# Other places for the operands and rounded weights of a decoder block's up-projection, in the order in which the last column pair uses them

## The chip, the core and the metric

The kernel runs on one core of one Trainium2 chip. The metric is device time in microseconds (us), the median over several executions; lower is better. The core's engines are named as in the profile: PE (TensorE, with its weight loads apart as PEld), DVE (VectorE), ACT (ScalarE), POOL (GpSimd) and SP (SyncE, which issues the DMAs). Each works through its own list of instructions in order and waits on semaphores for the others.

## The reference

One layer of a decoder block over 1024 tokens of width 1024: two token mixers in parallel, a residual and a layer norm, a gated feed-forward with a short causal convolution, a second norm, a gated embedding and a third norm.

```python
x = layer_norm(ALPHA * x + mixed, ln1_g, ln1_b)
h = causal_dwconv(x @ w_up, conv_w, conv_b)          # w_up: 1024 x 5632; three taps
h_gate, h_val = jnp.split(h, 2, axis=-1)             # 2816 columns each
ffn = (jax.nn.silu(h_gate) * h_val) @ w_down         # w_down: 2816 x 1024
x = layer_norm(ALPHA * x + ffn, ln2_g, ln2_b)
```

The change touches the product `x @ w_up`.

## The kernel before

**Two parts of each number.** A float32 operand is split into a rounded high part (`wh`, made by ACT at L101) and the remainder (`wl`, made by POOL or DVE at L106). A product of two operands is three matmuls: high by high, high by low, low by high (`mm3`, all at L155).

**Seven products in place of eight.** `x @ w_up` is cut in two by two blocks, and each pair of column blocks (a gate block of 128 columns and a value block) is computed by seven products of sums of blocks. There are 22 pairs, f = 0 to 21. For each product j there are an operand `XS[j]`, made once from the normed tokens in `x_sets` by `right_operands`, and for each pair a weight operand `W[j]`, made in `w_sets` by `left_operands`. A product is 4 by 3 matmuls on 128x512, a pair 84.

**How the weights are made.** Two raw blocks arrive by DMA, in tiles named `wr` for even pairs and `ar` for odd ones, four quarters a11, a12, a21, a22. `left_operands` forms on DVE (L164) the sums a11 = a11 - a21, a21 = a21 + a22, a22 = a22 - a11 and at last a12 = a12 - a22, all in place, and splits between them: product 0 is a11 as loaded, 5 is a22 as loaded, 1 is a22 after its sum, 2 is a21, 3 is a11 after its sum, 4 is a12 as loaded, 6 is a12 after its sum. Because the sums are in place, a sum must wait until the splits that read the old quarter are done: a12 waits for product 4's split, a22 for product 5's. From the second pair on every low part is made by POOL (`UE`), every high part by ACT.

**How a pair runs.** The functions in `up` are called in the order p0, p1, then p6 and the conv of the pair before, p5, p2, p3, p4, conv1. Results are collected in PSUM banks A to D (`ch`) and added into two tiles `h` (DVE at L1043, ACT at L1050 and L1074). p3 and p6 accumulate onto banks that p1 and p2 began, and must wait until DVE has read them. `conv` then scales on ACT (L1085), adds two taps on DVE (L1087), applies Silu on ACT (L1089), and POOL multiplies gate and value (L164 on `cv`, here called the gate product), whose result goes to DRAM (L1097).

**Places.** Tiles live in pools with a fixed number of places; a new tile of a pool's tag takes a place that an earlier tile of that tag has left, and its first write waits until the readers of that earlier tile are done. `bpool` has four places for `XS`, `apool[0]` two, `xpool` one. The weights' parts have four places each (`wh` and `wl`) in `wq` and three each in `fp`. When the 22 pairs are done, `xpool`, `wq`, `apool[0]` and `bpool` are closed, and `wpool` and `upool` of the down-projection are opened over the same bytes: units `wu` (weights) and `au` (activations), whose first writes wait for what lay there.

**What sets the order.** The code records instructions; a scheduler then sets the order on each engine, taking instructions as they become ready by its own reckoning and places as they become free. So other places can give another order.

Of the kernel before, what the change touches and what calls it, by code (L numbers as in the profile page):

```python
# [9 lines left out]
F32R = mybir.dt.float32r  # L10
# [7 lines left out]
P = 128  # L18
# [4 lines left out]
HALF = 512  # L23
# [17 lines left out]
def hybrid_block(ctx: ExitStack, tc: tile.TileContext, x, p, w_in, w_gate_up, b_gate, g_gla, w_gla,  # L41
# [5 lines left out]
    x, p, out = x[0], p[0, 0], out[0]  # L47
# [7 lines left out]
    def pool(name, bufs=1, space=bass.MemoryType.SB, stack=ctx, **kw):  # L55
        return stack.enter_context(tc.tile_pool(name=name, bufs=bufs, space=space, reuse_waits="tile", **kw))
# [5 lines left out]
    apool = [pool("acta", 2, stack=sega), pool("acta2", 2, stack=sega2, side="right")]  # L62
# [27 lines left out]
    def nm(s):  # L90
        uid[0] += 1
        return f"{s}_{uid[0]}"
# [122 lines left out]
    def quad(a):  # L215
        return a.rearrange("p (a b) -> p a b", b=P)
# [39 lines left out]
    def run(steps):  # L256
        for f in steps:
            f()
# [64 lines left out]
    with ExitStack() as mix:  # L323
# [65 lines left out]
        with ExitStack() as c1:  # L389
# [69 lines left out]
            def score_step(t, h):  # L459
                W = (t + 1) * P  # L460
                nch = 1 if W <= HALF else 2
                cw = W // nch
                sc = score[t]
# [219 lines left out]
        with ExitStack() as c3:  # L683
# [61 lines left out]
            def logit_steps(h, r):  # L745


                def one(i):
                    def f():
                        if i == 0:  # L750
                            PB[h, r] = tp.tile([P, 2 * r + 2, 2, 2, P], F16, name=nm("pt"), tag=f"pt{r}")
                        t, g = 2 * r + i, r // 2
                        W = (t + 1) * P
                        nch = 1 if W <= HALF else 2
                        cw = W // nch
                        qs = slice((t - g * 4) * P, (t - g * 4 + 1) * P)
# [83 lines left out]
    bpool = pool("actb", 4, stack=sega)  # L840
# [105 lines left out]
    segd, segk = ExitStack(), ExitStack()  # L946
    xpool = pool("xset", stack=segx)
    open_residual([x[t * P:(t + 1) * P, :] for t in range(NT)], 5)
    XS = [bpool.tile([P, 2, 4, HALF], F32R, name=nm("xs"), tag="B") for _ in range(4)]
    with ExitStack() as c1:  # L950
        lp = pool("ln1", stack=c1)
        gb1 = load_gb(lp, ln1_g, ln1_b)
        SPREAD, XE, XA = (1, 3), ('GVGVGVG', 'GVGVGVG', 'GGGVGGG', 'VVGVVGV'), ('VVVV', 'VVVV', 'VVVV', 'VVVG')

        def x_sets(i, xf):

            if i == 0:
                XS.extend(apool[0].tile([P, 2, 4, HALF], F32R, name=nm("xs"), tag="A") for _ in range(2))
                XS.append(xpool.tile([P, 2, 4, HALF], F32R, name=nm("xs"), tag="X"))
            cs = slice(i * P, (i + 1) * P)  # L960

            def put(j, src):
                split(XS[j][:, 0, :, cs], XS[j][:, 1, :, cs], quad(src), "A", XE[i][j])
            b11, b21, b12, b22 = xf
            run(right_operands(b11, b12, b21, b22, put, XA[i]))

        xfs = {}

        def fin1(t, nseg):
            layer_norm(t, nseg, gb1, EPS, t in SPREAD)  # L970
            r = RS["res"][t]
            tap(f"x1_{t}", r)
            xf = xfs.setdefault(t // 2, [])
            for g in range(2):
                pt = bank("mm" if t >= 4 else "pt", (P, 4, P))
                xq = lp.tile([P, HALF], F32, name=nm("xq"), tag="xq", bufs=5)
                xf.append(xq)
                for k in range(4):
                    n = g * 4 + k
                    turn_tile(pt[:, k], r[:, n * P:(n + 1) * P])  # L980
                S.activation(quad(xq), pt, AF.Copy)
            if t % 2:
                x_sets(t // 2, xf)
            nc.sync.dma_start(d_x1[t], r)

        def mixed(ps, rvs, *_):
            for j, rv in enumerate(rvs):
                V.scalar_tensor_tensor(rv, rv, ALPHA, ps[:, j], ALU.mult, ALU.add)

        tm_phase(FOURS, lambda c, *e: wload(wout_v, 0, KT, [c], *e),  # L990
                 lambda un, t, ps: tm_tile(un, tok(mT, t), ps),
                 mixed, fin1)
# [5 lines left out]
    with ExitStack() as c1:  # L998
        psum_banks(c1, "d", ch=8)
        fp = pool("ffwork", stack=c1)  # L1000
        rawp = pool("raws", stack=segd, side="right")
        wk = pool("upwork", stack=segk, side="right")
        UE, UE0, US = 'GGGGGGG', 'VVGVVGV', 'VVVV'
        nset = [0]

        def blocks(f):

            return (NF + f, f) if f < NF - 1 else (f, NF + f)

        def w_sets(f):  # L1010
            raw = []
            for c in blocks(f):
                if f % 2:
                    raw.append(rawp.tile([P, 6, 256], F32, name=nm("ar"), tag="ar", bufs=3)
                               .rearrange("p a b -> p (a b)")[:, :1024])
                else:
                    raw.append(wp.tile([P, 1024], F32, name=nm("wr"), tag="wr", bufs=2))
                nc.sync.dma_start(raw[-1].rearrange("p (k c) -> p k c", k=KT), wup_v[:, :, c * P:(c + 1) * P])
            W = []
            for _ in range(7):  # L1020
                n = nset[0] % 7
                nset[0] += 1
                pl, nb = (wq, 4) if n < 4 else (fp, 3)
                W.append([pl.tile([P, 512], F32R, name=nm(x), tag=x, bufs=nb) for x in ("wh", "wl")])
            run(left_operands(raw[1][:, :512], raw[1][:, 512:], raw[0][:, :512], raw[0][:, 512:],
                              lambda j, src: split(*W[j], src, "A", (UE if f else UE0)[j]), US))
            return [[quad(t) for t in w] for w in W]

        def up(f):

            W = w_sets(f)
            st, out_ = {}, {}

            def prod(ps, j, start):
                for k in range(4):
                    mm3(ps, (W[j][0][:, k], W[j][1][:, k]), (XS[j][:, 0, k], XS[j][:, 1, k]), start and k == 0, k == 3,
                        not start)  # L1040

            def plus(out, a, b):
                V.tensor_tensor(out=out, in0=a, in1=quad(b), op=ALU.add)  # L1043

            def p0():
                st["A"] = bank("ch")
                prod(st["A"], 0, True)
                st["h"] = [wk.tile([P, L], F32, name=nm("h"), tag=f"h{i}", bufs=2) for i in range(2)]
                st["hv"] = [h.rearrange("p (a g q) -> p g a q", g=2, q=P) for h in st["h"]]
                S.activation(st["hv"][1][:, 0], quad(st["A"]), AF.Copy)  # L1050

            def p1():
                st["B"] = bank("ch")
                prod(st["B"], 1, True)
                plus(st["hv"][0][:, 1], st["hv"][1][:, 0], st["B"])

            def p5():
                st["C"] = bank("ch")
                prod(st["C"], 5, True)

            def p2():
                st["D"] = bank("ch")
                prod(st["D"], 2, True)

            def p3():
                prod(st["B"], 3, False)
                s1, u3 = st["hv"][1][:, 0], st["hv"][1][:, 1]
                plus(u3, s1, st["B"])
                plus(s1, u3, st["C"])
                plus(u3, u3, st["D"])  # L1070

            def p4():
                prod(st["A"], 4, False)
                S.activation(st["hv"][0][:, 0], quad(st["A"]), AF.Copy)  # L1074

            def p6():
                prod(st["D"], 6, False)
                o = st["hv"][0][:, 1]
                plus(o, o, st["D"])

            def conv(i):
                c = blocks(f)[1 - i]
                h = st["h"][i]
                o = out_[c // NF] = wk.tile([P, L], F32, name=nm("cv"), tag="cv", bufs=3)
                S.activation(o, h, AF.Identity, bias=cbias[:, c:c + 1], scale=cw[:, 2, c:c + 1])  # L1085
                for d in (1, 2):
                    V.scalar_tensor_tensor(o[:, d:], h[:, :L - d], cw[:, 2 - d, c:c + 1], o[:, d:], ALU.mult, ALU.add)  # L1087
                if c < NF:
                    S.activation(o, o, AF.Silu)  # L1089

            def conv1():
                conv(1)

            def conv0():
                conv(0)
                sums(out_[0], out_[0], out_[1], ALU.mult, "G")
                nc.sync.dma_start(d_act[f // 6][:, f % 6], out_[0])  # L1097
            return p0, p1, p5, p2, p3, p4, conv1, p6, conv0

        late = []  # L1100
        for f in range(NF):
            p0, p1, p5, p2, p3, p4, conv1, *rest = up(f)
            run([p0, p1, *late[:1], p5, *late[1:], p2, p3, p4, conv1])
            late = rest
        late[0]()
        last_conv = late[1]
# [262 lines left out]
```

## Time and profile before

| what | value |
|---|---|
| median of 3 runs | 2147.39 us (2147.14 to 2148.36) |
| profiled execution, its own time | 2145.27 us |
| its span | 2143.6 us |
| mean granted PE clock | 0.984 of full speed |
| stretch of the up-projection's products | about 1295.6 to 1736.2 us |
| first down-projection matmul | 1736.5 us |

A row of the timeline gives start, duration, engine, line and operation, output and inputs with sizes, the count where rows were merged, and in brackets the engine's idle time before it with what ended it. Buffer numbers are left out in the profile's names. An instruction's duration includes time in which it is blocked after it was issued. A busy PE is not PE at its peak, since matmuls overlap.

### The profile page before, as it was taken

What the parts mean: (1) busy time and instruction counts of PE and PEld (TensorE: products, weight loads), DVE (VectorE), ACT (ScalarE), POOL (GpSimd) and SP (SyncE); (2) the same over time, 40 slices, a digit from 0 to 9 for tenths busy, and PEclk for the clock granted to TensorE, in tenths of its full rate; (3) what the DMA queues carried; (4) which work ended last, traced back from release to release, by engine and by line L of the source; (5) the groups of instructions that cost most, each with busy time, mean ns of one, the idle gap of its engine ahead of it and who ended that gap; (6) DMA issues with size and microseconds to landing.
All of it is one profiled execution on the core that took longest, in us unless ns stands there. A gap on an engine that the chain in (4) does not pass through costs nothing.

```text
span 2143.6 us, 32563 instructions
## 1 busy us (share of the span) xinstructions
PE 2063.3 (96%) x12210; PEld 1811.3 (84%) x12210; DVE 1564.6 (73%) x2742; ACT 846.0 (39%) x1540; POOL 1000.0 (47%) x832
## 2 busy tenths in 40 slices
PE   9999999999999999999999978999999979999997
PEld 8888899998988888887788976877777769989897
DVE  3589999999227888876234487777777788895965
ACT  4343312213126766675222244344344353342421
POOL 2423444535422121213231586776776684554753
PEclk9999999999999999999999998999999989999999
DMA  4322211211226686779766442222222134323222
GB/s 138 79 64 79 86 31 57 57 50 52 64 86 130 130 157 130 144 158 212 205 216 122 147 153 87 86 72 87 81 69 89 64 109 148 118 94 119 89 99 79
DMA packets 377566, 227.14 MB, mean 106 GB/s; under 512 B 189328, under 2 KB 351760, under 8 KB 377408
## 3 DMA queue, kind: packets, MB, share of 16 engines
q1 hardware_dynamic: 377408, 225.06, 38.7%
q8 instruction: 96, 1.57, 0.3%
q14 instruction: 62, 0.51, 0.1%
HBM read 146.37 MB, written 40.89 MB: 87 GB/s over the span
## 4 chain that ended last, share of the span: by engine, by line
PE 29%; DVE 9%; POOL 7%; issue 5%; DMA 3%; ACT 2%; SPq 0%; POOLq 0%; DVEq 0%; ACTq 0%
PE ch L155 16%; PE mm L155 13%; POOL wl L106 4%; DVE cv L1087 1%; DMA wr<-d_ob 1%; DVE cx L164 1%; DMA dr<-in_w_down_dram 1%; DVE h L1043 1%; ACT cv L1085 1%; DVE ar L164 1%; DVE wu L106 1%; DVE res_all L910 1%; DVE res_all L164 0%; DVE stats L933 0%; POOL lnmv L212 0%
## 5 line engine op out<-in xcount | busy, mean ns | idle before, releaser
L106 POOL TENSOR_TENSOR wl<-wr,wh 128x512 fp32r<-128x512 f32 x304 | 439.8, 1461 | 288.3 <-ACT wh L101 280.7
L155 PE MATMUL ch<-xs,wh 128*128 128x512 f32 x1232 | 384.8, 394 | 5.8 <-ACT wh L101 3.2
L155 PE MATMUL mm<-Ah,wh 128*128 128x512 f32 x832 | 332.1, 399 | 2.7 <-ACT wh L101 1.6
L155 PE MATMUL mm<-Al,wh 128*128 128x512 f32 x832 | 330.4, 397 | 0.3 <-POOL Al L106 0.3
L155 PE MATMUL mm<-Ah,wl 128*128 128x512 f32 x832 | 329.4, 396 | 0.0
L155 PEld LDWEIGHTS ch<-xs,wh 128*128 128x128 f32 x1232 | 231.5, 189 | 58.7 <-DVE h L1043 4.1
L103 POOL TENSOR_SCALAR wh<-wr 128x512 fp32r<-128x512 f32 x112 | 75.2, 674 | 381.1 <-PE mm L155 194.4
L155 PE MATMUL ch<-xs,wl 128*128 128x512 f32 x616 | 242.8, 395 | 6.8 <-POOL wl L106 6.7
L155 PE MATMUL mm<-wl,Ah 128*128 128x256 f32 x768 | 217.1, 284 | 5.2 <-POOL wl L106 5.1
L155 PE MATMUL mm<-wh,Al 128*128 128x256 f32 x768 | 215.8, 283 | 0.0
L155 PE MATMUL ch<-wu,au 128*128 128x256 f32 x1512 | 194.0, 292 | 22.5 <-DVE au L106 7.2
L155 PE MATMUL mm<-wh,Ah 128*128 128x256 f32 x768 | 213.2, 283 | 0.0
L1087 DVE SCALAR_TENSOR_TENSOR cv<-h,cw,cv 128x1023 f32<-128x1023 f32 x88 | 168.6, 1915 | 60.0 <-ACT cv L1085 58.5
L155 PEld LDWEIGHTS ch<-wu,au 128*128 128x128 f32 x1512 | 190.4, 199 | 25.9 <-DVE au L106 8.1
L101 ACT ACTIVATE wh<-wr 128x512 fp32r<-128x512 f32 (+1 forms) x201 | 120.5, 623 | 194.7 <-PE mm L155 81.6
L155 PEld LDWEIGHTS mm<-Ah,wh 128*128 128x128 f32 x832 | 156.7, 188 | 33.4 <-ACT wh L101 2.1
L155 PEld LDWEIGHTS mm<-Ah,wl 128*128 128x128 f32 x832 | 156.4, 188 | 33.0
L155 PEld LDWEIGHTS mm<-Al,wh 128*128 128x128 f32 x832 | 156.5, 188 | 30.7 <-POOL Al L106 0.8
L674 DVE MATCH_REPLACE8 score<-m,score 128x896 f32<-128x896 f32 (+3 forms) x192 | 166.5, 869 | 0.0
L673 DVE MAX8 m<-score 128x8 f32<-128x896 f32 (+3 forms) x192 | 163.6, 876 | 2.3 <-POOL score L480 2.1
L155 PEld LDWEIGHTS mm<-wl,Ah 128*128 128x128 f32 x768 | 145.1, 189 | 7.1 <-POOL wl L106 6.4
L155 PEld LDWEIGHTS ch<-xs,wl 128*128 128x128 f32 x616 | 116.5, 189 | 38.2 <-POOL wl L106 14.0
(269 smaller groups left out, 4328.4 us busy)
## 6 DMA issues: line engine op xcount, KB each, us to landing
wr<-in_w_in_dram SPq DMA_DIRECT2D x60, 512.0 KB, 3.8
wr<-in_w_up_dram SPq DMA_DIRECT2D x22, 512.0 KB, 3.9
ar<-in_w_up_dram SPq DMA_DIRECT2D x22, 512.0 KB, 4.0
d_act<-cv SPq DMA_DIRECT2D x22, 512.0 KB, 2.6
dr<-in_w_down_dram SPq DMA_DIRECT2D x12, 768.0 KB, 7.0
ar<-d_act SPq DMA_DIRECT2D x12, 768.0 KB, 5.1
d_tg<-tg SPq DMA_DIRECT2D x32, 256.0 KB, 2.0
wr<-in_w_out_dram SPq DMA_DIRECT2D x16, 512.0 KB, 3.6
```

The costliest lines, as they stand in the source:

```text
L101: S.activation(dst, src, AF.Copy, scale=scale)
L103: (V if eng == "V" else G).tensor_scalar(dst, src, scale, 0.0, ALU.mult, ALU.add)
L106: done["GV"[eng != "G"]] = (G if eng == "G" else V).tensor_tensor(out=dst, in0=src, in1=hi.bitcast(F32), op=ALU.subtract)
L155: T.matmul(ps, lhsT=l, rhs=r, start=start, stop=stop, skip_group_check=more)
L164: (G if eng == "G" else V).tensor_tensor(out=out, in0=a, in1=b, op=op)
L673: V.max(m8, score[t])
L674: V.match_replace(score[t], m8, score[t], TAKEN)
L910: V.scalar_tensor_tensor(r[:, a:b], r[:, a:b], mv[:, 2:3], gb[1][:, a:b], ALU.mult, ALU.add)
L1043: V.tensor_tensor(out=out, in0=a, in1=quad(b), op=ALU.add)
L1085: S.activation(o, h, AF.Identity, bias=cbias[:, c:c + 1], scale=cw[:, 2, c:c + 1])
L1087: V.scalar_tensor_tensor(o[:, d:], h[:, :L - d], cw[:, 2 - d, c:c + 1], o[:, d:], ALU.mult, ALU.add)
```

## The change

The operands `XS` and the weights' parts `W` are handed out in another order, with the product's number as key of a dictionary in place of a list. Before, `bpool` held the operands of products 0, 1, 2 and 3, `apool[0]` those of 4 and 5, `xpool` that of 6. Now `bpool` holds 5, 2, 3 and 4, `apool[0]` holds 0 and 1, `xpool` 6. Before, the parts of products 0, 1, 2, 3 shared `wq`'s places and 4, 5, 6 shared those of `fp`. Now 0, 1, 5, 2 share `wq` and 3, 4, 6 share `fp`: the order of the products in a pair. What is computed, and the number of instructions, stay as they were. Lines after the edit are three lower than before (L1043 is L1040, L1085 is L1082, L1087 is L1084).

```diff
-    XS = [bpool.tile([P, 2, 4, HALF], F32R, name=nm("xs"), tag="B") for _ in range(4)]
+    XS = {j: bpool.tile([P, 2, 4, HALF], F32R, name=nm("xs"), tag="B") for j in (5, 2, 3, 4)}
...
             if i == 0:
-                XS.extend(apool[0].tile([P, 2, 4, HALF], F32R, name=nm("xs"), tag="A") for _ in range(2))
-                XS.append(xpool.tile([P, 2, 4, HALF], F32R, name=nm("xs"), tag="X"))
+                for j, (pl, tag) in enumerate(((apool[0], "A"), (apool[0], "A"), (xpool, "X"))):
+                    XS[(0, 1, 6)[j]] = pl.tile([P, 2, 4, HALF], F32R, name=nm("xs"), tag=tag)
...
-        nset = [0]
...
-            W = []
-            for _ in range(7):
-                n = nset[0] % 7
-                nset[0] += 1
+            W = {}
+            for n, j in enumerate((0, 1, 5, 2, 3, 4, 6)):
                 pl, nb = (wq, 4) if n < 4 else (fp, 3)
-                W.append([pl.tile([P, 512], F32R, name=nm(x), tag=x, bufs=nb) for x in ("wh", "wl")])
+                W[j] = [pl.tile([P, 512], F32R, name=nm(x), tag=x, bufs=nb) for x in ("wh", "wl")]
...
-            return [[quad(t) for t in w] for w in W]
+            return {j: [quad(t) for t in w] for j, w in W.items()}
```

The order on the engines moves in every pair in the same way; two places show it, both in the middle of the up-projection, around pairs 11 and 12.

On POOL, from one gate product to the next, before. The gate products are the rows on `cv`. Tiles `ar_146..` are the raw blocks of pair 11, `wr_1475.` those of pair 12. The rows in between split products 1, 2, 3, 4 of pair 11, then 0 of pair 12, 6 of pair 11 and 5 of pair 12:

```order
L164 TENSOR_TENSOR cv_14554<-cv_14554,cv_14458 128x1024
L106 TENSOR_TENSOR wl_14613<-ar_14606,wh_14612 128x512
L106 TENSOR_TENSOR wl_14615<-ar_14606,wh_14614 128x512
L106 TENSOR_TENSOR wl_14617<-ar_14608,wh_14616 128x512
L106 TENSOR_TENSOR wl_14619<-ar_14608,wh_14618 128x512
L106 TENSOR_TENSOR wl_14755<-wr_14752,wh_14754 128x512
L106 TENSOR_TENSOR wl_14623<-ar_14608,wh_14622 128x512
L106 TENSOR_TENSOR wl_14765<-wr_14750,wh_14764 128x512
L164 TENSOR_TENSOR cv_14698<-cv_14698,cv_14602 128x1024
```

The same stretch of POOL now. Numbers of the parts follow the new order of handing out, so that product 5 of pair 12 is `wl_14759` and product 1 of it `wl_14757`; the rows are products 2, 3, 4 of pair 11, 0 and 5 of pair 12, 6 of pair 11, 1 of pair 12:

```order
L164 TENSOR_TENSOR cv_14554<-cv_14554,cv_14458 128x1024
L106 TENSOR_TENSOR wl_14617<-ar_14606,wh_14616 128x512
L106 TENSOR_TENSOR wl_14619<-ar_14608,wh_14618 128x512
L106 TENSOR_TENSOR wl_14621<-ar_14608,wh_14620 128x512
L106 TENSOR_TENSOR wl_14755<-wr_14752,wh_14754 128x512
L106 TENSOR_TENSOR wl_14759<-wr_14750,wh_14758 128x512
L106 TENSOR_TENSOR wl_14623<-ar_14608,wh_14622 128x512
L106 TENSOR_TENSOR wl_14757<-wr_14750,wh_14756 128x512
L164 TENSOR_TENSOR cv_14698<-cv_14698,cv_14602 128x1024
```

Product 5's split moved up behind product 0's, and product 1's split of the next pair moved from behind the gate product to ahead of it.

On DVE in the same place, before: the sum a12 of pair 11, the sums a11 and a21 of pair 12, the additions to `h` after product 1 of pair 12 and after product 6 of pair 11, the two taps of pair 11's convolution, and the sum a22 of pair 12:

```order
L164 TENSOR_TENSOR ar_14608<-ar_14608,ar_14606 128x512
L164 TENSOR_TENSOR wr_14752<-wr_14752,wr_14750 128x512
L164 TENSOR_TENSOR wr_14750<-wr_14750 128x512
L1043 TENSOR_TENSOR h_14655<-h_14656,ch_14658 128x4x128
L1043 TENSOR_TENSOR h_14511<-h_14511,ch_14561 128x4x128
L1087 SCALAR_TENSOR_TENSOR cv_14698<-h_14511,cw,cv_14698 128x1023
L1087 SCALAR_TENSOR_TENSOR cv_14698<-h_14511,cw,cv_14698 128x1022
L164 TENSOR_TENSOR wr_14750<-wr_14750,wr_14752 128x512
```

The same rows of DVE now:

```order
L164 TENSOR_TENSOR ar_14608<-ar_14608,ar_14606 128x512
L164 TENSOR_TENSOR wr_14752<-wr_14752,wr_14750 128x512
L164 TENSOR_TENSOR wr_14750<-wr_14750 128x512
L1040 TENSOR_TENSOR h_14655<-h_14656,ch_14658 128x4x128
L164 TENSOR_TENSOR wr_14750<-wr_14750,wr_14752 128x512
L1040 TENSOR_TENSOR h_14511<-h_14511,ch_14561 128x4x128
L1084 SCALAR_TENSOR_TENSOR cv_14698<-h_14511,cw,cv_14698 128x1023
L1084 SCALAR_TENSOR_TENSOR cv_14698<-h_14511,cw,cv_14698 128x1022
```

The sum a22 moved from behind the convolution to between the two additions to `h`. On ACT the rounding for product 5 moved likewise, ahead of product 6's, and that for product 1 ahead of the Silu.

## Prediction

> **What bounds the kernel now.** I read the page's head, then the busy time by stretch, then what the matmul engine waited for, then the order of time on the vector engines inside one column pair.
>
> ```profile
> span 2143.6 us, 32563 instructions
> PE 2063.3 (96%) x12210; PEld 1811.3 (84%) x12210; DVE 1564.6 (73%) x2742; ACT 846.0 (39%) x1540; POOL 1000.0 (47%) x832
> ```
>
> PE looks busy everywhere, but pipelined matmuls hide short waits, so I count them per stretch. The columns are length, then busy time and count on PE, PEld, DVE, ACT and POOL, then granted clock, DMA share and GB/s.
>
> ```profile
> 1340.00:1360.00 20.00, 20.00 (x90) 16.57 (x89) 14.69 (x14) 8.45 (x13) 14.21 (x9) 1.00 0.25 79
> 1360.00:1700.00 340.00, 333.62 (x1443) 268.19 (x1442) 249.43 (x222) 141.63 (x208) 241.49 (x138) 1.00 0.26 82
> ```
>
> Both stretches lie in the up-projection at full clock. The first shows 90 matmuls in 20 us (88 if two reach over its edges), so a pair's 84 need 18.7 to 19.1 us. The second shows 1443 in 340 us, 19.8 us for 84. Some 0.8 us a pair is lost. To whom, the waits between 1290 and 1736 us tell:
>
> ```profile
> PE ch L155 <- POOL wl L106: 6.7, 16, 0.6
> ```
>
> One wait in each of sixteen pairs, for a low part that POOL splits. First and last of them on PE:
>
> ```profile
> 1420.44 0.50 PE L155 MATMUL ch<-xs,wl 128*128 128x512 f32 x1 [0.41 <-POOL wl L106]
> 1718.88 0.50 PE L155 MATMUL ch<-xs,wl 128*128 128x512 f32 x1 [0.41 <-POOL wl L106]
> ```
>
> They lie 298.44 us apart, fifteen steps of 19.90. The wait first shows after five pairs, so something off PE runs at 19.9 from the start and PE catches up with it. POOL in one period, with the first and the last gate product (L164 on `cv`) around it:
>
> ```profile
> 1337.16 2.41 POOL L164 TENSOR_TENSOR cv<-cv,cv 128x1024 f32<-128x1024 f32 x1 [3.59 <-ACT cv L1089]
> ...
> 1376.94 2.41 POOL L164 TENSOR_TENSOR cv<-cv,cv 128x1024 f32<-128x1024 f32 x1 [2.38 <-ACT cv L1089]
> 1379.30 7.03 POOL L106 TENSOR_TENSOR wl<-wr,wh 128x512 fp32r<-128x512 f32 x4
> 1386.29 1.29 POOL L106 TENSOR_TENSOR wl<-ar,wh 128x512 fp32r<-128x512 f32 x1
> 1388.92 1.68 POOL L106 TENSOR_TENSOR wl<-wr,wh 128x512 fp32r<-128x512 f32 x1 [1.35 <-ACT wh L101]
> 1392.66 1.81 POOL L106 TENSOR_TENSOR wl<-ar,wh 128x512 fp32r<-128x512 f32 x1 [2.06 <-ACT wh L101]
> 1396.84 2.41 POOL L164 TENSOR_TENSOR cv<-cv,cv 128x1024 f32<-128x1024 f32 x1 [2.37 <-issue]
> ...
> 1715.16 2.42 POOL L164 TENSOR_TENSOR cv<-cv,cv 128x1024 f32<-128x1024 f32 x1 [2.37 <-issue]
> ```
>
> Gate product to gate product: 378.00 us in nineteen periods, 19.89 each, from the first on. After it come the splits of products 1 to 4, then those of product 0 (next pair), 6, and 5 (next pair). DVE and ACT in the same period:
>
> ```profile
> 1386.36 1.76 DVE L164 TENSOR_TENSOR wr<-wr,wr 128x512 f32<-128x512 f32 x1 [2.44 <-POOL wl L106]
> 1388.04 0.68 DVE L164 TENSOR_TENSOR ar<-ar,ar 128x512 f32<-128x512 f32 x1
> 1388.76 0.69 DVE L164 TENSOR_TENSOR ar<-ar 128x512 f32<-128x512 f32 x1
> 1389.37 1.28 DVE L1043 TENSOR_TENSOR h<-h,ch 128x512 f32<-128x512 f32 x2
> 1392.04 3.51 DVE L1087 SCALAR_TENSOR_TENSOR cv<-h,cw,cv 128x1023 f32<-128x1023 f32 x2 [1.40 <-ACT cv L1085]
> 1395.47 0.68 DVE L164 TENSOR_TENSOR ar<-ar,ar 128x512 f32<-128x512 f32 x1
> ```
>
> ```profile
> 1388.21 0.63 ACT L101 ACTIVATE wh<-wr 128x512 fp32r<-128x512 f32 x1 [6.64 <-DVE wr L164]
> 1390.76 1.24 ACT L1085 ACTIVATE cv<-h,cbias,cw 128x1024 f32<-128x1024 f32 x1 [1.92 <-DVE h L1043]
> 1391.91 0.62 ACT L101 ACTIVATE wh<-ar 128x512 fp32r<-128x512 f32 x1
> 1395.64 1.06 ACT L1089 ACTIVATE cv<-cv 128x1024 f32<-128x1024 f32 x1 [3.12 <-DVE cv L1087]
> ```
>
> This is a closed ring without PE: gate product; four splits to 1386.33; the sum a12 (it waits for product 4's split); the sums a11 and a21 of the next pair; two additions to h; ACT's scaling; two convolution steps to 1395.55; Silu to 1396.70; gate product at 1396.84. **The ring is the bound: 19.9 us a pair against PE's 19.1.**
>
> **What the change does, part by part.** No instruction is added or dropped; places change hands, and with them the order on the engines. Inside the loop three things move (the order's rows are above).
>
> First, product 1's split goes ahead of the gate product and leaves the ring. Four splits took 7.03 us; the last three alone:
>
> ```profile
> 1479.95 5.76 POOL wl L106 x3
> ```
>
> That takes off 1.27 us. PE's wait for it goes too; it was a symptom of the ring.
>
> Second, product 5's split now stands directly behind product 0's, where POOL had paused 1.35 us, and product 6's behind that. DVE's a12 already shows the price of meeting a split: issued 0.07 us behind product 0's, it took 1.76 us, where a11, with POOL idle, took 0.68. With POOL busy without a pause, a11 and a21 meet splits as well. Product 6's is ready in time, since its rounding on ACT (0.63 us) starts as soon as a12 is done. The additions to h keep their 1.28 us beside a running split, as they do now. The trace has one place with back-to-back splits and sums of this size, first on POOL, then on DVE:
>
> ```profile
> 1306.47 1.73 POOL L106 TENSOR_TENSOR xs<-xq,xs 128x512 fp32r<-128x512 f32 x1
> 1308.15 1.74 POOL L106 TENSOR_TENSOR wl<-ar,wh 128x512 fp32r<-128x512 f32 x1
> ```
>
> ```profile
> 1305.82 2.93 DVE L106 TENSOR_TENSOR wl<-wr,wh 128x512 fp32r<-128x512 f32 x2 [0.46 <-ACT wh L101]
> ```
>
> There DVE needs 1.47 us each, 0.79 over 0.68; a12 is 1.08 over it. Both rows are of the same size and kind, so I take the middle, 0.94, twice: 1.88 us. Below, it could be 0 (POOL never in the way).
>
> Third, the sum a22 moves from behind the convolution (1395.47) to between the two additions to h, into the ring. It lasts 0.68 and overlaps its neighbour by 0.08 as a11 does with a12: 0.60 us. What is queued behind it on DVE is product 6's addition to h and the convolution; ACT's scaling and so the gate product wait for these.
>
> Unchanged: the convolution meets one split now (product 5's, 1.81) and one afterwards (product 1's), so 3.51 stays. Sum of the ring: -1.27 + 1.88 + 0.60 = +1.21 us, a period of 21.1.
>
> Does PE feel it? Product 3 accumulates onto the bank that the first addition to h reads, and waits for that already:
>
> ```profile
> 1708.43 0.30 PEld L155 LDWEIGHTS ch<-xs,wh 128*128 128x128 f32 x2 [0.23 <-DVE h L1043]
> ```
>
> So no cover is left there: the longer ring goes to PE, as a wait of some 2.0 us (21.1 less 19.1) before product 3. The few microseconds of lead that PE has in the first pairs are spent in both kernels. Over nineteen periods: 19 x 1.21 = **+23.0 us**.
>
> At the stage's start PE waits for a rounding that the new places may let come sooner or later:
>
> ```profile
> 1304.27 2.69 PE L155 MATMUL ch<-xs,wh 128*128 128x512 f32 x5 [3.17 <-ACT wh L101]
> ```
>
> The operands' own sums and roundings feed it, in whatever place; I take 0 and keep -3.2 to +3.2. In the last pair product 1's earlier split may give 1.3 back; taken as 0.
>
> At the end of the stage lies the place that the change names: down-projection splits go into places that now are free earlier. PE's waits there, and the stretch's busy times:
>
> ```profile
> 1738.82 0.39 PE L155 MATMUL ch<-wu,au 128*128 128x256 f32 x1 [2.02 <-POOL wu L106]
> 1740.10 3.16 PE L155 MATMUL ch<-wu,au 128*128 128x256 f32 x16 [0.89 <-POOL au L106]
> 1749.74 11.96 PE L155 MATMUL ch<-wu,au 128*128 128x256 f32 x74 [6.49 <-ACT au L101]
> 1764.91 7.28 PE L155 MATMUL ch<-wu,au 128*128 128x256 f32 x46 [3.22 <-POOL au L106]
> ```
>
> ```profile
> 1736.40:1767.50 31.10, 18.48 (x107) 16.90 (x106) 31.03 (x44) 19.09 (x42) 28.55 (x24) 0.75 0.31 102
> ```
>
> There are 12.62 us of waits, but DVE is busy 31.03 of 31.10 us: it forms the sums that these splits read, in its own order, and no place makes it faster. I take 0; bounds 0 and -12.6.
>
> The profiled execution would come to 2145.27 + 23.0 = 2168.3 us (its span 2143.6, and 1.67 around it); it lies 2.1 under the median of the runs, 2147.39, so the forecast is **2170.4 us**.
>
> **Rivals.**
>
> *The sums don't meet the splits* (other side: faster). If POOL and DVE alternate so that a11 and a21 stay at 0.68, the ring is 19.89 - 1.27 + 0.60 = 19.2 us, near PE's own 19.1. Nineteen times 0.67 is 12.7 us: **2134.7**. It decides from a surcharge under 0.67 us for both sums together. For it: two of the three sums run at 0.68 today. Against: they do so while POOL pauses, and that pause is gone. Chance 0.10.
>
> *Each sum waits out a whole split.* Then a11 and a21 each pay a split's full 1.29 us on top of their own, whenever they were issued: 2.58 in place of 1.88, the ring +1.91, 36.3 us in all: **2183.7**. Against: neither row of today pays that much; they pay 0.79 and 1.08. Chance 0.04. This is what the Trainium skill's page "SBUF — State Buffer", section "SBUF: two separate sides", would make of it: a VectorE instruction with two SBUF inputs and a GpSimd instruction share one port pair, which whoever starts first holds for its whole length while the other blocks. The trace agrees in kind, and its two sizes stay below the rule's.
>
> *Only one of the two meets a split*, product 6's coming late. Ring +0.27, 5 us in all: **2152.5**. The margin is small, a few tenths between rounding and split. Chance 0.10.
>
> *The earlier places are worth their waits after all*: all 12.6 us at the down-projection's start come back, beside the longer ring: **2157.8**. DVE's full stretch speaks against it. Chance 0.06.
>
> *The clock.* A wait of 2 us in each pair could cost clock. After the row with 2.47 us idle, the next stretch shows 0.83:
>
> ```profile
> 1829.22 1.99 PE L155 MATMUL ch<-wu,au 128*128 128x256 f32 x11 [2.47 <-DVE au L106]
> ```
>
> ```profile
> 1830.00:1840.00 10.00, 9.69 (x67) 9.36 (x66) 9.44 (x17) 6.30 (x15) 8.46 (x8) 0.83 0.73 238
> ```
>
> A clock of 0.83 over 10 us is 1.7 us of matmuls lost, 32 in nineteen pairs, **2202**. But PE then only reaches its wait 1.7 us later, and the wait of 2.0 shrinks by it; the ring doesn't care. Chance 0.02. The Trainium skill's page "TensorE: Matmul & The Clock Gate", section "HAM oscillation — how this bites in real kernels", asks only that idle gaps stay under about 3.4 us, and would give this rival no room; the row with 2.47 us disagrees.
>
> *The change does nothing measurable*, the new order being absorbed: **2147.4**. Against: the ring has no slack. Chance 0.02.
>
> **The numbers.** The forecast has 0.66. The range reaches from the one-split rival, 2152, to both sums at 1.08 and a22 at 0.68 (ring +1.57, 29.8 us) with 3.2 us at the start, 2180; it leaves out 0.18: the faster rival, the whole splits, the clock and no effect. A measurement of this kernel can tell about 0.2%, 4.3 us. Faster: 0.10. Slower: 0.66 for the forecast, 0.04 for whole splits, 0.06 of the one-split rival, 0.06 for the places and 0.02 for the clock, 0.84. Same: the rest of that rival and no effect, 0.06.
>
> **What would show it.** Right: gate products 21 us apart; PE waiting about 2 us for an addition to h (L1040 then) in every pair, and no longer for a split; the sums a11 and a21 near 1.6 us; three splits in a row on POOL. The start of the down-projection keeps its waits and DVE its full stretch. Wrong in the ring: periods under 19.9 us with a11 and a21 at 0.7. Wrong at the end: the 6.49 us wait gone.

## The result, and the profile after

The changed kernel takes **2176.32 us** (median of 4 runs, 2175.60 to 2178.63); the kernel before, on the same chip, 2147.44 (2147.14 to 2148.36). The ratio is 1.0136, with a 95% interval of 1.0118 to 1.0153: slower by 28.9 us. The forecast was 2170.4, in a range of 2152 to 2180. Of the runs in the table further down, one of experiment 5 took 3400.06 us at a granted clock of 0.555 in place of 0.98; it counts in the median there, but not in the ratio.

The head of the page after, and the busy time of the loop (columns as in the prediction: length, then PE, PEld, DVE, ACT, POOL with their counts, clock, DMA share, GB/s):

```profile
span 2174.3 us, 32587 instructions
PE 2069.7 (95%) x12210; PEld 1817.4 (84%) x12210; DVE 1590.8 (73%) x2742; ACT 845.2 (39%) x1540; POOL 1006.2 (46%) x832
```

```profile
1360.00:1700.00 340.00, 315.23 (x1343) 255.01 (x1342) 254.91 (x209) 130.56 (x192) 233.68 (x128) 0.98 0.23 75
```

In 340 us PE now does 1343 matmuls where it did 1443. What it waits for, from 1290 to 1736 us, and three pairs of it on PE:

```profile
PE ch L155 <- DVE h L1040: 27.5, 18, 2.0
```

```profile
1377.95 0.73 PE L155 MATMUL ch<-xs,wh 128*128 128x512 f32 x2 [1.94 <-DVE h L1040]
1399.25 0.73 PE L155 MATMUL ch<-xs,wh 128*128 128x512 f32 x2 [0.36 <-DVE h L1040]
1420.53 0.72 PE L155 MATMUL ch<-xs,wh 128*128 128x512 f32 x2 [1.92 <-DVE h L1040]
```

The columns of the first row are the sum of the waits, their number and the longest. The wait for a split is gone; the wait of product 3 for an addition to `h` has taken its place, with 1.9 us in most pairs. The order of time on POOL over one period, with the first and the last gate product of the loop around it:

```profile
1342.67 2.41 POOL L164 TENSOR_TENSOR cv<-cv,cv 128x1024 f32<-128x1024 f32 x1 [3.59 <-ACT cv L1086]
...
1385.29 2.40 POOL L164 TENSOR_TENSOR cv<-cv,cv 128x1024 f32<-128x1024 f32 x1 [2.38 <-ACT cv L1086]
1387.65 5.75 POOL L106 TENSOR_TENSOR wl<-wr,wh 128x512 fp32r<-128x512 f32 x3
1393.36 2.99 POOL L106 TENSOR_TENSOR wl<-ar,wh 128x512 fp32r<-128x512 f32 x2
1396.31 1.74 POOL L106 TENSOR_TENSOR wl<-wr,wh 128x512 fp32r<-128x512 f32 x1
1402.35 1.87 POOL L106 TENSOR_TENSOR wl<-ar,wh 128x512 fp32r<-128x512 f32 x1 [4.30 <-PE ch L155]
1406.59 2.42 POOL L164 TENSOR_TENSOR cv<-cv,cv 128x1024 f32<-128x1024 f32 x1 [2.37 <-issue]
...
1747.26 2.42 POOL L164 TENSOR_TENSOR cv<-cv,cv 128x1024 f32<-128x1024 f32 x1 [2.36 <-PE ch L155]
```

From the first to the last are 404.59 us, nineteen periods of 21.29. Behind the gate product come six splits without a pause: products 2, 3, 4, then 0 and 5 of the next pair, then 6; product 1's stands ahead of the next gate product. DVE in the same period:

```profile
1393.44 1.76 DVE L164 TENSOR_TENSOR wr<-wr,wr 128x512 f32<-128x512 f32 x1 [2.44 <-POOL wl L106]
1395.12 1.78 DVE L164 TENSOR_TENSOR ar<-ar,ar 128x512 f32<-128x512 f32 x1
1396.93 1.66 DVE L164 TENSOR_TENSOR ar<-ar 128x512 f32<-128x512 f32 x1
1398.52 0.67 DVE L1040 TENSOR_TENSOR h<-h,ch 128x512 f32<-128x512 f32 x1
1399.12 0.68 DVE L164 TENSOR_TENSOR ar<-ar,ar 128x512 f32<-128x512 f32 x1
1399.72 0.67 DVE L1040 TENSOR_TENSOR h<-h,ch 128x512 f32<-128x512 f32 x1
1401.79 3.51 DVE L1084 SCALAR_TENSOR_TENSOR cv<-h,cw,cv 128x1023 f32<-128x1023 f32 x2 [1.39 <-ACT cv L1082]
```

The sums a11 and a21, 0.68 and 0.69 us before, take 1.78 and 1.66; a22 stands between the additions. One slip of the text ahead of the prediction: by the names in the order, the additions to `h` and the taps shown there belong to pairs 11 and 10, one pair earlier than it says. No step of the sum hangs on it.

**Where the 30.7 us of the profiled execution lie** (spans 2143.6 and 2174.3). First gate product: 1342.67 against 1337.16, +5.51. Nineteen periods: 404.59 against 378.00, +26.59. From the twentieth gate product to the end: 427.04 against 428.44, -1.40. Together +30.70.

Of the 5.51, 3.74 are there at the stage's first product, which starts at 1299.35 where it started at 1295.61:

```profile
1299.35 1.22 PE L155 MATMUL ch<-xs,wh 128*128 128x512 f32 x2 [2.60 <-DVE xq L164]
```

The ring's row of sums stands once ahead of the first gate product, and it is already longer there. The sum a12 and ACT's scaling behind the row, before and now, with the sums a11 and a21 between them now:

```profile
1325.34 1.77 DVE L164 TENSOR_TENSOR ar<-ar,ar 128x512 f32<-128x512 f32 x1
1329.85 1.24 ACT L1085 ACTIVATE cv<-h,cbias,cw 128x1024 f32<-128x1024 f32 x1 [0.38 <-DVE h L1043]
```

```profile
1328.69 1.78 DVE L164 TENSOR_TENSOR ar<-ar,ar 128x512 f32<-128x512 f32 x1
1330.40 1.78 DVE L164 TENSOR_TENSOR wr<-wr,wr 128x512 f32<-128x512 f32 x1
...
1332.70 1.18 DVE L164 TENSOR_TENSOR wr<-wr 128x512 f32<-128x512 f32 x1
...
1335.37 1.24 ACT L1082 ACTIVATE cv<-h,cbias,cw 128x1024 f32<-128x1024 f32 x1 [3.47 <-DVE h L1040]
```

The sum a12 starts 3.35 us later, and from it to the scaling are 6.68 us in place of 4.51, +2.17. From the scaling to the gate product nothing changes (7.30 and 7.31).

The start of the down-projection, at which the exchanged places come free:

```profile
1768.90 1.75 PE L155 MATMUL ch<-wu,au 128*128 128x256 f32 x11
1771.26 1.09 PE L155 MATMUL ch<-wu,au 128*128 128x256 f32 x7 [0.60 <-POOL au L106]
1781.21 10.21 PE L155 MATMUL ch<-wu,au 128*128 128x256 f32 x65 [8.86 <-ACT au L101]
```

The wait for the weights' unit (2.02 us before) is gone, but the wait for the activations' unit has grown from 6.49 to 8.86. Up to that unit PE stands 9.46 us instead of 9.40. The wait of 3.22 us that came next is replaced by five shorter ones up to 1799.54, 2.77 us together, so that the start of the down-projection has 12.23 us of waits where it had 12.62.

### The profile page after: what moved, and what is told of

Read it like the earlier page. It is cut to its first block, busy times and chain, and to the rows that moved or that the text cites. A ratio compares the mean times of both kernels' runs of the same rounds, so it can differ in the third digit from the quotient of the medians.

```text
span 2174.3 us, 32587 instructions
## 1 busy us (share of the span) xinstructions
PE 2069.7 (95%) x12210; PEld 1817.4 (84%) x12210; DVE 1590.8 (73%) x2742; ACT 845.2 (39%) x1540; POOL 1006.2 (46%) x832
## 4 chain that ended last, share of the span: by engine, by line
PE 28%; DVE 11%; POOL 5%; issue 5%; DMA 2%; ACT 2%; SPq 0%; POOLq 0%; DVEq 0%; ACTq 0%
PE ch L155 15%; PE mm L155 13%; POOL wl L106 4%; DVE ar L164 2%; DVE cx L164 1%; DVE wr L164 1%; ACT wh L101 1%; DVE h L1040 1%; DVE au L106 1%; DMA wr<-d_ob 1%; DVE wu L106 1%; DVE res_all L164 1%; DVE res_all L910 1%; DVE um L164 0%; DVE cv L1084 0%
## 5 line engine op out<-in xcount | busy, mean ns | idle before, releaser
L106 POOL TENSOR_TENSOR wl<-wr,wh 128x512 fp32r<-128x512 f32 x304 | 444.4, 1475 | 297.3 <-ACT wh L101 272.5
L155 PE MATMUL ch<-xs,wh 128*128 128x512 f32 x1232 | 390.8, 399 | 35.1 <-DVE h L1040 29.4
L1084 DVE SCALAR_TENSOR_TENSOR cv<-h,cw,cv 128x1023 f32<-128x1023 f32 x88 | 155.0, 1762 | 61.2 <-ACT cv L1082 59.7
L106 POOL TENSOR_TENSOR wl<-ar,wh 128x512 fp32r<-128x512 f32 x77 | 133.1, 1743 | 55.0 <-ACT wh L101 39.9
```

The source lines that it names most:

```text
L106: done["GV"[eng != "G"]] = (G if eng == "G" else V).tensor_tensor(out=dst, in0=src, in1=hi.bitcast(F32), op=ALU.subtract)
L155: T.matmul(ps, lhsT=l, rhs=r, start=start, stop=stop, skip_group_check=more)
```

## The experiments

Each kernel was timed in 3 rounds (the last in 5) beside the kernel before, whose median in that series was 2146.62 us for experiments 1 to 4, 2145.95 for 5 to 8 and 2147.47 for 9; the ratios are to that series. The period is that between gate products over the loop, from first and twentieth; where the first pairs differ from the rest, that of the later pairs.

| kernel | time, us | ratio (95%) | period, us |
|---|---|---|---|
| before | 2147.44 | | 19.89 |
| changed | 2176.32 | 1.0136 (1.0118 to 1.0153) | 21.29 |
| 1, weights only | 2175.57 | 1.0132 (1.0117 to 1.0147) | 21.30 |
| 2, operands only | 2150.31 | 1.0016 (1.0007 to 1.0025) | 19.90 |
| 3, changed, 5 behind 6 | 2132.73 | 0.9937 (0.9920 to 0.9954) | 19.04 |
| 4, before, op in the pause | 2181.82 | 1.0162 (1.0147 to 1.0177) | 21.65 |
| 5, before, one-input op | 2173.78 | 1.0118 (1.0098 to 1.0139) | 21.23 |
| 6, changed, 1 behind gate | 2182.96 | 1.0170 (1.0155 to 1.0186) | 21.56 |
| 7, before, 4 on DVE | 2132.25 | 0.9935 (0.9920 to 0.9950) | 19.09 |
| 8, before, 6 recorded late | 2133.53 | 0.9939 (0.9924 to 0.9953) | 19.04 |
| 9, as 3, norm first | 2130.69 | 0.9921 (0.9908 to 0.9935) | 19.04 |

The theory is that of the prediction: the loop is a ring of POOL, DVE and ACT; the new places only make the scheduler choose another order, and in this order two sums meet splits. The rivals: that the operands' places do it; that instructions wait for places; that the sums are longer for another reason than the splits beside them.

### 1 and 2: one half of the change at a time

Against the changed kernel, experiment 1 gives the operands their old places:

```diff
-    XS = {j: bpool.tile([P, 2, 4, HALF], F32R, name=nm("xs"), tag="B") for j in (5, 2, 3, 4)}
+    XS = {j: bpool.tile([P, 2, 4, HALF], F32R, name=nm("xs"), tag="B") for j in (0, 1, 2, 3)}
...
-                    XS[(0, 1, 6)[j]] = pl.tile([P, 2, 4, HALF], F32R, name=nm("xs"), tag=tag)
+                    XS[(4, 5, 6)[j]] = pl.tile([P, 2, 4, HALF], F32R, name=nm("xs"), tag=tag)
```

Experiment 2 gives the weights their old ones:

```diff
-            for n, j in enumerate((0, 1, 5, 2, 3, 4, 6)):
+            for n, j in enumerate((0, 1, 2, 3, 4, 5, 6)):
```

> The kernel before with only the weights' half of the change (products 0, 1, 5, 2 share one pool's places, 3, 4, 6 the other's); the operands XS keep their old places. Ring theory (the time is made by the loop's order on POOL and DVE, and only the weights' places set that order): gate products 21.3 us apart, the sums a11 and a21 at 1.65 to 1.8 us, PE waiting 1.9 us for an addition to h in most pairs; the time 2172 to 2177 us, where the lower end leaves to the operands the 3.7 us by which the first product starts later in the changed kernel. Rival, operands theory (the places of XS make the loop slow or the start late): gate products 19.9 us apart, 2145 to 2150 us.

> The kernel before with only the operands' half of the change (XS[0] and XS[1] in apool, XS[5], 2, 3, 4 in bpool). Ring theory: the loop only reads XS, its order stays, gate products 19.9 us apart; the time 2143 to 2152 us, the bounds being what the start of the stage may gain or lose. Operands theory: 21.3 us apart and some 2176 us. A third, that both halves are needed for the new order, would show here 19.9 and in the run with the weights alone 19.9 as well.

The weights alone give the whole of it: 2175.57 us, a period of 21.30, the same wait of 2.0 us for `h`, and the late start too (first product at 1299.44). The operands alone leave the period at 19.90. Their 2150.31 is 3.7 us over the 2146.62 of the kernel before in that series: the first product starts 1.72 us later (1297.33). In the profiled execution (span 2146.2, 2.6 over that of before) 1.68 us of this reach the first gate product, and 0.90 arise behind the twentieth; why is open. The operands theory falls.

### 3: the changed kernel, product 5's split behind product 6's

```diff
...
+            if j == 5 and f > 1:
+                with tc.issue_after(low[6, f - 1].ins):
+                    split(*W[j], src, "A", UE[j])
...
```

`low` holds POOL's split of each product and pair.

> The changed kernel, all its places kept, with one edge added: POOL's split of product 5 is queued behind its split of product 6 of the pair before. Ring theory: POOL's pause behind product 0's split returns, a11 and a21 take 0.68 us each (2.07 us less), and the splits of products 1 and 2 both come ahead of the gate product, so the ring falls to about 17 us and PE's own 19.05 us bounds the loop. Nineteen periods at 0.84 us under before's 19.89: 2131 us, up to 2136 with the later start of the changed kernel; faster than both. Rival, places theory (the loop is slow because roundings and splits wait for the places that the change gives them, whatever the order): the places are the same, so 21.3 us apart and 2172 to 2177 us.

Measured 2132.73 us, faster than both. POOL and DVE in one period of it:

```profile
1437.34 1.29 POOL L106 TENSOR_TENSOR wl<-ar,wh 128x512 fp32r<-128x512 f32 x1
1438.89 1.96 POOL L106 TENSOR_TENSOR wl<-ar,wh 128x512 fp32r<-128x512 f32 x1 [0.26 <-ACT wh L101]
1440.86 2.22 POOL L106 TENSOR_TENSOR wl<-wr,wh 128x512 fp32r<-128x512 f32 x1
1446.25 1.30 POOL L106 TENSOR_TENSOR wl<-ar,wh 128x512 fp32r<-128x512 f32 x1 [3.17 <-ACT wh L101]
```

```profile
1441.86 1.77 DVE L164 TENSOR_TENSOR ar<-ar,ar 128x512 f32<-128x512 f32 x1
1443.56 0.68 DVE L164 TENSOR_TENSOR wr<-wr,wr 128x512 f32<-128x512 f32 x1
1444.27 0.69 DVE L164 TENSOR_TENSOR wr<-wr 128x512 f32<-128x512 f32 x1
```

Three splits follow the gate product (3, 4 and product 0 of the next pair), then POOL pauses for 3.17 us, and the two sums fall into the pause at 0.68 and 0.69 us. The busy time shows the new bound, PE without a gap:

```profile
1360.00:1700.00 340.00, 340.00 (x1502) 281.53 (x1501) 246.20 (x233) 156.10 (x215) 234.22 (x143) 1.00 0.25 82
```

All places of the change are kept, so waiting for places is not what makes the changed kernel slow. The order is.

### 4 and 5: one more POOL instruction in the old kernel's pause

Directly behind product 0's split, product 0's low part is multiplied by one in place, in 4 with a second input in SBUF, in 5 with one input only.

Experiment 4:

```diff
...
+            if j == 0 and f:
+                with tc.issue_after(done["G"].ins):
+                    G.tensor_tensor(out=W[0][1], in0=W[0][1].bitcast(F32), in1=ones1.to_broadcast([P, 512]), op=ALU.mult)
...
```

Experiment 5 has this as the last line:

```diff
...
+                    G.tensor_scalar(W[0][1], W[0][1].bitcast(F32), 1.0, 0.0, ALU.mult, ALU.add)
...
```

> The kernel before with one more POOL instruction in each pair from the second on: product 0's low part is multiplied by one, in place, directly behind its split; the result is unchanged. It fills POOL's pause of 1.35 us. Contention theory (a DVE sum with both inputs in SBUF and a POOL instruction of that kind keep each other waiting): a11 and a21 now meet a running instruction each and take 1.6 to 1.8 us in place of 0.68, the ring grows by 1.9 to 2.1 us to 21.8 to 22.0, and PE waits some 2.7 us a pair; nineteen to twenty periods make it 2184 to 2190 us. Rival (the sums of the changed kernel are longer for another reason, such as where their tiles lie or what they wait for): 1.28 us fit into a pause of 1.35, the ring stays 19.9 and the time 2147 to 2150 us.

Measured 2181.82 us, 35.2 over the 2146.62 of before in that series and 2 us under the expected range; the period 21.65, +1.76. The instruction on POOL, and the two sums on DVE:

```profile
1436.22 1.37 POOL L1014 TENSOR_TENSOR wl<-wl,ones 128x512 fp32r<-128x512 f32 x1
```

```profile
1436.61 1.52 DVE L164 TENSOR_TENSOR ar<-ar,ar 128x512 f32<-128x512 f32 x1
1438.17 1.65 DVE L164 TENSOR_TENSOR ar<-ar 128x512 f32<-128x512 f32 x1
```

The sums grow by 0.84 and 0.96 us, 1.80 together, and the period by 1.76. No place and no product was moved. A POOL instruction beside the sums is enough to reproduce the changed kernel's long sums.

> As the run with an instruction in POOL's pause, but the instruction is a tensor_scalar (times one, plus zero) with a single input in SBUF; such a one takes POOL 0.67 us in the profile of before (75.2 us over 112). If only POOL instructions with two SBUF inputs and DVE sums keep each other waiting, a11 and a21 stay at 0.68 us, the ring at 19.9 and the time at 2147 (2145 to 2150). If any POOL instruction in SBUF does, a11 alone meets it and waits up to 0.67 us: the ring 20.3 to 20.6, the time 2155 to 2161 us.

Neither case came: 2173.78 us, a period of 21.23.

```profile
1433.28 0.94 POOL L1014 TENSOR_SCALAR wl<-wl 128x512 fp32r<-128x512 f32 x1
1434.55 1.35 POOL L106 TENSOR_TENSOR wl<-wr,wh 128x512 fp32r<-128x512 f32 x1 [0.33 <-ACT wh L101]
```

```profile
1433.66 1.09 DVE L164 TENSOR_TENSOR ar<-ar,ar 128x512 f32<-128x512 f32 x1
1434.79 1.66 DVE L164 TENSOR_TENSOR ar<-ar 128x512 f32<-128x512 f32 x1
```

An instruction with one input does hold up the sum a11, by 0.41 us. The expectation stopped there. But now a21 is issued 0.24 us after product 6's split began, where in the kernel before it was issued 0.16 us ahead of it (1388.76 against 1388.92), and it pays 0.97. The two make 1.38, and the period grew by 1.34. So the old order was fast by a margin of 0.16 us.

### 6: the term of product 1

```diff
...
+            if j == 1 and f > 2:
+                with tc.issue_after(gates[f - 2].ins):
+                    split(*W[j], src, "A", UE[j])
...
```

`gates` holds the gate products. The changed kernel otherwise.

> The changed kernel with one edge added: POOL's split of product 1 is queued behind the gate product of two pairs before, where it stood in the kernel before. This prices the term of -1.27 us. Ring theory: four splits stand in the ring again (+1.27), and a11 and a21 still meet splits. With product 1's split gone from beside the convolution, the two steps should take 2.60 in place of 3.50 us (-0.90), which the prediction's sum did not consider: a ring of 21.3 + 1.27 - 0.90 = 21.7, 2183 us; without that discount 22.6, 2200 us. If the split's place is of no account, 21.3 and 2176 us.

Measured 2182.96 us and 21.56. That the time hits the expected 2183 is partly luck: the period stayed under 21.7, but the first gate product came 1.76 us later than in the changed kernel, and the end took 1.13 more. The two taps take 2.60 us with no split beside them, as expected:

```profile
1425.70 2.60 DVE L1093 SCALAR_TENSOR_TENSOR cv<-h,cw,cv 128x1023 f32<-128x1023 f32 x2 [1.38 <-ACT cv L1091]
```

So taking a split out of the row behind the gate product is worth its 1.27 us only as long as it does not land beside the convolution where none stood; here it nets 0.27.

### 7 and 8: the ring taken off in the old places

Experiment 7, against the kernel before:

```diff
-        UE, UE0, US = 'GGGGGGG', 'VVGVVGV', 'VVVV'
+        UE, UE0, US = 'GGGGVGG', 'VVGVVGV', 'VVVV'
```

Experiment 8, against the kernel before; `steps` are what `left_operands` returns, and its last is product 6's split:

```diff
...
+            if 0 < f < NF - 1:
+                held.append(steps.pop())
+            if f > 1:
+                steps.insert(3, held.pop(0))
...
```

> The kernel before with product 4's low part made by DVE in place of POOL, from the second pair on. Ring theory: the sum a12 then waits for no POOL split, the ring falls under 19.05 us and PE's own 84 matmuls bound the loop: gate products 19.05 apart, nineteen times 0.84 us less, 2131 us (2129 to 2134), though DVE has more to do. Rival (PE lost its 0.8 us a pair to the waits for product 1's low part or to something else that no ring explains): 2145 to 2150 us, gate products 19.9 apart.

> The kernel before, all its places kept, with the roundings of product 6 recorded in the next pair's set, behind product 5's; a22's sum then goes ahead of the convolution as in the changed kernel, and products 1 and 2 are split ahead of the gate product, but product 5's rounding comes late on ACT, so that POOL pauses behind product 0's split. Ring theory: a11 and a21 at 0.68 us, the ring under 19.05, PE bounds: 2131 us (2129 to 2135). It says that the order alone, in the old places, gives what the changed kernel with product 5 behind product 6 gave. Rival (the gain of that run needs the changed places): 19.9, 2147 us.

Measured 2132.25 us with 19.09, and 2133.53 with 19.04. In 7 DVE has more to do (290.07 us of the 340 in place of 249.43) and the kernel is faster; that it was the ring and not DVE's load that cost PE its 0.8 us a pair is shown. In 8 no place differs from the kernel before, and the time is that of experiment 3, whose places are those of the change. The last gate products of the loop in 7 and 8, the twentieth:

```profile
1700.61 2.41 POOL L164 TENSOR_TENSOR cv<-cv,cv 128x1024 f32<-128x1024 f32 x1 [2.37 <-issue]
```

```profile
1699.33 2.40 POOL L164 TENSOR_TENSOR cv<-cv,cv 128x1024 f32<-128x1024 f32 x1
```

### 9: the late start

In the changed kernel DVE forms a22 of the very first pair at 1288.30 and splits product 1 at 1292.79, between the last steps of the layer norm (1288.90 and 1293.39). This run is experiment 3 with an edge that puts them behind.

```diff
...
+            run(steps[:4])
+            with ExitStack() if f else tc.issue_after(done["norm"].ins):
+                run(steps[4:])
...
```

> The changed kernel with product 5 split behind product 6 (the run that measured 2132.73 us, first product at 1299.32 us of its span), and with a second edge: the sum a22 of the very first pair, and what DVE does for that pair after it, stand behind DVE's last step of the layer norm. In the changed kernel that sum (0.68 us) and product 1's low part (0.68 us) lie ahead of the last two norm steps on DVE, and the first product starts 3.74 us later than in the kernel before. If these two instructions, and what they meet on POOL, are what delays the norm, the first product starts at 1296 to 1298 and the time is 2129.5 to 2132 us, the fastest so far. If the delay comes from elsewhere ahead of them (DVE had already fallen some 1 us behind by 1280 us), the first product stays at 1299 and the time at 2132 to 2134 us. In both cases the gate products stay 19.05 us apart.

The time, 2130.69, lies in the expected range but cannot be told from experiment 3's, since the intervals overlap; and the mechanism missed. In the profiled execution (at 2133.53 the slowest of its five) the last transposes start earlier (1292.84, 1294.79 in experiment 3), but the first product starts later (1301.84, 1299.32 in experiment 3):

```profile
1292.84 1.94 PE L88 MATMUL mm<-ident,res 128*128 128x128 f32 x8 [2.13 <-DVE res L910]
1301.84 1.22 PE L155 MATMUL ch<-xs,wh 128*128 128x512 f32 x2 [7.05 <-ACT xq L981]
```

ACT copies the transposed tokens only then, behind a rounding that waits for a DVE sum. The edge moved ACT's order as well. What makes the start late stays open; that it comes with the weights' places is shown by experiment 1, though the operands' places alone (experiment 2) delay it by 1.72 us too.

## Why the prediction was right

**What bounds the kernel: right.** The ring bounded it. Experiments 7 and 8 take the ring off, and PE's own time appears, 19.04 to 19.09 us a pair, as the prediction read it from 88 to 90 matmuls in 20 us (18.7 to 19.1). One reading is off by one: the first wait for a split, at 1420.44, stands in the seventh pair, behind six pairs and not five. Nothing hangs on it.

**The sum of the ring: right in each term, a little small.** Starts compared with starts in the rows of both kernels:

| step | predicted, us | measured, us | from |
|---|---|---|---|
| product 1's split leaves the row | -1.27 | -1.27 | three splits 5.75, four 7.03 |
| a11 and a21 meet splits | +1.88 | +2.07 | a11 1.81 to the next start in place of 0.72, a21 1.59 in place of 0.61 |
| a22 between the additions | +0.60 | +0.60 | 1399.12 to 1399.72 |
| ring | +1.21 | +1.40 | 21.29 less 19.89 |

The mis-sized term is the middle one. The prediction took the mean of two rows, 0.79 and 1.08 over 0.68; both sums paid near the upper, 1.09 and 0.98. The rows say why: with POOL never pausing, sum and split take turns. Split 5 is issued at 1394.61 and lasts until 1396.36; a11, issued at 1395.12, ends at 1396.90, 0.5 us behind it. Split 6 is issued at 1396.31 and lasts until 1398.05; a21 ends at 1398.59, 0.5 us behind it. Each sum waits out the split that runs beside it, and the next split waits for the sum. The upper row, a12 issued just behind a split, was this very case. The lower one is a mean of two instructions, of which the first (1.24 us) was issued 1.00 us behind its split and so had less of it to wait for. The Trainium skill's page "SBUF — State Buffer", section "SBUF: two separate sides", has the two share one port pair that is held for a whole instruction. The turns agree with that; the 2.58 us that the prediction worked out from it for both sums is more than the 2.07 measured, because it took a full split for each sum, and a sum waits only for what is left of its split.

**PE and the cover: right.** The wait of product 3 for `h` took the place of that for the split, 1.9 us predicted as 2.0; nineteen periods gave 26.6 in place of 23.0.

**The start: outside the bounds.** The prediction held -3.2 to +3.2 us and took 0; the first gate product came 5.51 late. This is the step that failed, in two ways. The stage's first product came 3.74 us late, where the prediction had looked only at the one wait of 3.17 us behind it; 3.35 of this reached the sum a12 of the first period. And the ring's longer row, 2.17 us there, acts once before the first gate product, where the prediction counted nineteen periods only. Why the first product is late stays open. Of the 7.7 us by which the profiled execution lies beyond the forecast of 23.0, it makes 5.5, the ring 3.6, and the end -1.4.

**The end: right.** DVE stayed full (32.16 of the 32.30 us from 1767.20 to 1799.50), and the waits at the down-projection stayed, 12.23 us in place of 12.62. That the one is the cause of the other is argued, not tested; from the twentieth gate product on the changed kernel gained 1.40 us of the 12.6 that were at stake.

**The rivals.** That the sums don't meet the splits needs POOL's pause; experiments 3 and 8 restored it, and with it came the faster side, 2133 instead of the 2134.7 of that rival. *Each sum waits out a whole split* is, in kind, what the rows show; its price of 1.29 us was too high, since from start to start a split cost the sums 1.09 and 0.98. *Only one of the two meets a split* asks that product 6's split come later than a21; it was issued at 1396.31, 0.62 us ahead of a21, and experiment 5, which put one short instruction beside a11, has a21 meet that split as well. *The earlier places are worth their waits* did not come: 0.4 of the 12.6 us of waits went.

**The clock** did what the prediction said it would do. In every fourth pair or so the wait is short (0.36 above), and the stretch ahead of it shows a lower clock:

```profile
1364.00:1385.00 21.00, 19.06 (x78) 15.26 (x77) 15.69 (x14) 7.86 (x12) 14.61 (x8) 0.92 0.24 76
1385.00:1406.00 21.00, 20.64 (x92) 16.74 (x91) 15.67 (x14) 7.96 (x13) 14.63 (x8) 1.00 0.24 76
```

PE loses some 1.7 us to the clock (8% of 21) and waits 1.6 us less; the gate products stay 21.29 apart.

## What to carry to other kernels

Where a scheduler orders the work, a change of places is a change of order: compare the order first, find the ring in the loop, and price each instruction that enters or leaves it. A pause of an engine that is off the bound can be what keeps a neighbour fast; ask what fills it. And where a change loses by the order alone, one edge may turn it: the changed places with product 5's split held behind product 6's run at 0.9937 of the kernel before, where without it they run at 1.0136.

## What the runs showed of the hardware

A POOL instruction with a single SBUF input also holds up a DVE sum: a11 took 1.09 us beside it in place of 0.68, and the instruction itself 0.94 us (mean of 19), where such ones take 0.67 us in the profile of before.

Behind waits of 1.94 us on PE a lower clock showed. This is the stretch of 2 us that begins 2 us after the wait that ended at 1377.95:

```profile
1380.00:1382.00 2.00, 2.00 (x7) 1.52 (x6) 1.48 (x2) 0.98 (x2) 0.94 (x1) 0.50 0.01 2
```

It does not follow each wait: of nineteen stretches of one period five show 0.92, the others 1.00. In experiment 4, whose waits for `h` in the loop are 1.7 us at most, the 340 us from 1360 to 1700 show 1.00. The Trainium skill's page "TensorE: Matmul & The Clock Gate", section "HAM oscillation — how this bites in real kernels", asks for gaps under about 3.4 us. These gaps are shorter, and the row disagrees.
